# Feed-forward block products on Trainium2: one 512-column product for the high weights, and block products from an earlier pair

## The chip, the cores and the metric

The kernel runs on one core of one Trainium2 chip, in one launch. The metric is the device time of that launch in microseconds. Three runs of the kernel before took 1226.37, 1226.70 and 1227.45 us, median 1226.7. Shares, waits and durations come from one profiled execution of the same kernel. Engines are named as the profile has them: PE is TensorE (PEld its weight loads), DVE is VectorE, ACT is ScalarE, POOL is GpSimd, SP is SyncE, whose queue issues most of the DMAs.

## What is computed

Two layers of a decoder trunk on one sequence of 512 positions, 1024 wide, in float32. Layer 0 mixes tokens by a stick-breaking attention, layer 1 by a sparse attention that selects keys. Each layer ends in the gated feed-forward that the change is about:

```python
def conv_ffn(h, w_up, conv_w, conv_b, w_down):      # h (1, 512, 1024)
    S = h.shape[1]
    u = h @ w_up                                    # (1024, 2 * 2816)
    up = jnp.pad(u, ((0, 0), (CONV_W - 1, 0), (0, 0)))
    y = conv_b
    for j in range(CONV_W):
        y = y + up[:, j:j + S] * conv_w[j]
    gate, val = jnp.split(y, 2, axis=-1)
    return (jax.nn.silu(gate) * val) @ w_down       # (2816, 1024)
...
mod = cond @ ada_w[i] + ada_b[i]
sh1, sc1, g1, sh2, sc2, g2 = [m[:, None, :] for m in jnp.split(mod, 6, axis=-1)]
...
h = rms_norm(x, norm_ffn[i]) * (1.0 + sc2) + sh2
x = x + g2 * conv_ffn(h, ffn_w_up[i], ffn_conv_w[i], ffn_conv_b[i], ffn_w_down[i])
```

## The kernel before

**Numbers in two parts.** Every float32 operand of a large product is split into a high part (rounded to the matmul's type, `whi`, `hhi`, `thi`, `acthi`, `dnhi`) and the rest (`wlo`, `hlo`, ...). A product is three: high weight with high input, high weight with low input, low weight with high input. The high part of a weight is a ScalarE copy. The low part is either a VectorE subtraction, or a negated ScalarE copy onto which an accumulating DMA, issued by POOL, adds the float32 weight again (`neg_...`, `add_...`).

**Pairs.** Each feed-forward has 22 pairs j = 0 to 21: 128 columns of the gate half and 128 of the value half of `w_up`. A plain pair (`up_plain`, `plain_hi` and `plain_lo`, L1525 and L1529) makes two products of 512 positions: for each of the halves 8 row tiles of the weight times three, 48 matmuls of 512 columns.

**Seven products.** From pair `FIRST_7` on (12 in the first feed-forward, 7 in the second) a pair is made by seven block products in place of eight (`up_7`, `product`, L1549). The input is cut into four blocks, two halves of the 1024 features by two halves of 256 positions, the weight into four, two halves of the rows by gate and value. Sums of weight blocks (`sum13`, `sum24a`, `sum24b`) and of input blocks (the combinations T, `combos`, once per feed-forward) make seven products a1, a2, e, d1, d2, c1, c2. Each is 4 row tiles times three, 12 matmuls of 256 columns. They accumulate in three PSUM banks, and are read out between products: bank a takes a1, e, c1 and c2 on top of one another, and after a1 a ScalarE copy takes the gate's first half (`gate` 0), after e another copy (`x`), after c1 a VectorE addition (`val` 1), and after c2 a copy (`gate` 2). Bank b holds a2 (`gate` 1), bank d holds d1 and then d2 (`v`, and `val` 0). So a product that accumulates onto a bank has to wait until the one before has been read. The block's result then goes through scale, two convolution steps, silu and a multiplication into A[j].

**Down products.** `w_down` is multiplied in rounds over pairs 0-5, 6-11, 12-17 and 18-21. The first three rounds make 24 down products (`down`, L1624): six pairs of A times three, 18 matmuls of 512 columns, added to x by VectorE (L744). `DOWNS_7` says after which pair how many of them stand. In the seven-product pairs one stands between c1 and c2, so that TensorE has work while VectorE reads bank a, and the rest of them after c2.

**Dots.** The modulation vectors `mod` are computed on VectorE: 8 dots per vector (`dot`, L651) over loaded 512 KB chunks of `ada_w`, spread over the work as fillers. A bias (`bias_job`) takes one of the shift vectors out to DRAM, reads it back on all partitions (`shrow`), and makes two more dots with weight columns.

**What sets the order.** `ffn_plan` lists the jobs of a feed-forward with an estimated duration each, keeps TensorE's jobs in the order of the program, gives every other job a latest time by what waits for it, and runs a list schedule over the engines and the ring buffers. The result is the order in which instructions are issued. Each engine then works through its queue in that order and waits at semaphores. Tables steer the plan: `FIRST_7`, `DOWNS_7`, `ORDER_7` (the order of products in a pair), `PLAIN_DMA` and `DOWN_DMA` (which low parts come by accumulating DMA), `DOT_SPAN` and `LEADS`. Float32 weights are loaded into a ring of six `raw` buffers by SP.

Of the kernel before, what the change touches and what calls it, by code (L numbers as in the profile page):

```python
# [19 lines left out]
S = 512  # L20
P = 128
# [40 lines left out]
FIRST_7 = [12, 7]  # L62
DOWNS_7 = [[(6, 1), (7, 2), (8, 1), (9, 1), (10, 1), (11, 1), (12, 2), (13, 1), (14, 2), (15, 1), (16, 1), (17, 1), (18, 2),
            (19, 2), (20, 2), (21, 3)],
           [(6, 2), (7, 1), (8, 1), (9, 1), (10, 1), (11, 1), (12, 2), (13, 1), (14, 2), (15, 1), (16, 1), (17, 1), (18, 2),
            (19, 2), (20, 2), (21, 3)]]
ORDER_7 = ["a1", "d1", "a2", "e", "d2", "c1", "down", "c2", "rest"]
WEIGHT_7 = {"a1": 0, "d2": 0, "a2": 1, "d1": 13, "c1": 13, "e": 24, "c2": 24}
BANK_7 = {"a1": "a", "e": "a", "c1": "a", "c2": "a", "a2": "b", "d1": "d", "d2": "d"}
LATE_CHUNKS = [(2, 3), ()]  # L70
A_RING = 11
BIAS_AT = [16, 20, 26, 30]
LATE_DOTS = True
DOT_SPAN = [(0.0, 300.0), (5.0, 60.0)]
PLAIN_DMA = [(), [(j, i) for j in range(4, 7) for i in range(2)]]
DOWN_DMA = [(), ()]
LEADS = [dict(plain=14.0, r=20.0, sum=13.0, down=12.0, T=28.0, last=12.0, bias=2.0)] * 2
# [116 lines left out]
def ffn_dots(l):  # L194
    groups = [[(0, 5), (1, 0), (1, 3), (1, 1), (1, 2), (1, 4)] + ([] if LATE_DOTS else [(1, 5)]), [(1, 5)] if LATE_DOTS else []][l]
    jobs = [g + (f,) for g in groups for f in range(KT)]
    if l == 0:
        for n, at in zip((1, 1, 2, 2), BIAS_AT):
            jobs.insert(at, ("bias", n, "row" if ("bias", n, "col") in jobs else "col"))
    return jobs  # L200


def ffn_plan(l):
# [112 lines left out]
    def up_7(j, downs):  # L316
# [19 lines left out]
        done = {}  # L336
        for what in ORDER_7:
            if what in ("down", "rest"):
                for i in downs[:1] if what == "down" else downs:
                    down(i)  # L340
                downs = downs[1:]
                continue
            need = [done[n] for n in {"e": ["g0"], "d2": ["v"], "c1": ["x"], "c2": ["v1"]}.get(what, [])]
# [3 lines left out]
            m1 = p.add("PE", 8 * 0.12, "prod_hi", j, what, after=[hi] + need)  # L347
# [5 lines left out]
            if bank not in done:  # L353
                done[bank] = p.place("x" if what == "a2" else "mm", m1)

            def after(name, engine, us, fn, arg, *needs):
                if name not in done and all(n in done for n in needs):
                    done[name] = p.add(engine, us, fn, j, arg, after=[done[n] for n in needs])
                    return True

            if after("g0", "ACT", 0.38, "gate", 0, "a1"):
                gate = p.place("u", done["g0"])
            after("g1", "DVE", 0.42, "gate", 1, "g0", "a2")
            if after("v", "ACT", 0.38, "copy", "v", "d1"):
                small = p.place("sqt", done["v"])
            after("x", "ACT", 0.38, "copy", "x", "e", "v")
            if after("v1", "DVE", 0.42, "val", 1, "v", "c1"):
                val = p.place("u", done["v1"])
            after("v0", "DVE", 0.42, "val", 0, "x", "d2", "v1")
            after("g2", "ACT", 0.38, "gate", 2, "c2")  # L370
        small.users += [done["v1"], done["v0"]]
        done["bank a"].users.append(done["g2"])
        done["bank b"].users.append(done["g1"])
        done["bank d"].users.append(done["v0"])
        v = evacuate(j, 1, [done["v0"], done["v1"]])
        g = evacuate(j, 0, [done["g1"], done["g2"]])
        gate.users.append(g[0])
        val.users.append(v[0])
        mix(j, g, v)

    def down(i):
# [13 lines left out]
        bank = p.place("z" if m % 2 else "tr", m1)  # L395
        m2 = p.add("PE", 6 * 0.2266, "down", i, 1, after=[lo])
        w.users.append(m2)
        for j in ins:
            A[j][2].users.append(m2)
        bank.users.append(p.add("DVE", 0.75, "add", i, after=[m2] + gate_done))  # L400

    gate_done = []
# [3 lines left out]
    for d in jobs:  # L406
# [21 lines left out]
    assert n == 3 * KT  # L428
    for j in range(2, FT):
        if j == first:  # L430
            combos(p.t)
        if j >= first:
            up_7(j, downs.get(j, ()))
        else:
            up_plain(j)
            for i in downs.get(j, ()):
                down(i)
# [59 lines left out]
def kernel_body(ctx, tc, xT, wst, cst, smalls, crow, ccol, relb, outT):  # L497
# [126 lines left out]
    ada_cap = len(ada_jobs)  # L624
    tail = [(0, 5, f) for f in range(KT)] + [(1, g, f) for g in (1, 0, 3, 2, 4, 5) for f in range(KT)]
    for n, at in ((1, 29), (2, 42)):
        for d, what in ((0, "col"), (4, "row")):
            tail.insert(at + d, ("bias", n, what))
    ada_jobs += tail
    ada_state = {"i": 0, "cap": ada_cap}  # L630
# [130 lines left out]
    def boundary(n, last, O, l, gate, nxt, first, place, begin=None):  # L761

# [4 lines left out]
        norm_scale(nl, gcol, sc)  # L767
        fetch(pos["i"] + 1)
# [101 lines left out]
    def stick_layer(l):  # L870
        with ExitStack() as st:
# [497 lines left out]
            ada_finish()  # L1369
            ada_state["cap"] = len(ada_jobs)  # L1370
# [17 lines left out]
    def ffn_layer(l, first, man):  # L1388
        with ExitStack() as st:
# [45 lines left out]
            class do:  # L1435
# [66 lines left out]
                def combo_hi(k):  # L1502
                    T[k] = [fp.tile([P, 3 * H2], F32R, name=n, bufs=4) for n in ("thi", "tlo")]
# [69 lines left out]
                def val(j, i):  # L1573
                    if i == 1:
                        Y[j, "val"] = npool.tile([P, S], F32, name="val", tag="u", bufs=3)
                        dve.tensor_add(Y[j, "val"][:, H2:], half[j][:, :H2], pt[j, "a"])
# [800 lines left out]
```

## Time and profile before

| | us |
|---|---|
| median of three runs | 1226.7 |
| the profiled execution's own time | 1226.43 |
| its span, first to last instruction | 1224.6 |
| POOL busy | 171.2 |
| first feed-forward on TensorE | 280.3 to 588.1 |
| second feed-forward on TensorE | 894.9 to 1199.3 |

The page of the profile gives each engine's busy time, the chain of work that ended last, and the costliest groups of instructions. A row of a group names the line, the engine, the operation, output and input tiles with partitions x elements, and the count; behind the first bar the busy time in us and the mean ns of one, behind the second the idle time of the engine just before these instructions and what ended it. In rows in order of time the first number is the start, the second how long it took, both in us from the span's start, and a bracket gives the idle time ahead of it and what ended that. [...] Here are the totals that the prediction does not show again, of ScalarE's and VectorE's waits in the second feed-forward's seven-product part (957 to 1191 us):

```profile
ACT vx L1562 <- PE pt_a L1549: 26.1, 15, 2.5
...
DVE raw L1474 <- ACT whi L1442: 10.6, 10, 2.4
...
DVE x L744 <- PE pt_d L1624: 6.0, 12, 1.1
```

The three numbers are the total in us, how often, and the longest: both engines wait there for TensorE and for each other.

### The profile page before, as it was taken

The page shows a single profiled execution, that of the slowest core. Times are in us where ns is not written, and L with a number is a line of the kernel's source. Part 1 is how long each engine was busy: PE and PEld are TensorE (multiplying, and loading weights), DVE is VectorE, ACT ScalarE, POOL GpSimd, SP SyncE. Part 2 cuts the span into 40 slices and gives each one's busy share as a digit, 9 for nine tenths or more (in the row PEclk, how much of TensorE's full clock was granted, in tenths as well). Part 3 has the DMA queues.
Part 4 walks back from the last instruction along what each step waited for, and adds up shares of the span by engine and source line. Part 5 has one row for each costly group of instructions (what it writes and reads, how often), then busy time and mean ns, then how long its engine had stood idle before and what let it go on. Part 6 is the DMA issues. An engine that isn't in the chain of part 4 may idle for free.

```text
span 1224.6 us, 18659 instructions
## 1 busy us (share of the span) xinstructions
PE 1218.8 (100%) x6924; PEld 1036.2 (85%) x6924; DVE 1029.9 (84%) x1715; ACT 736.9 (60%) x1265; POOL 171.2 (14%) x187
## 2 busy tenths in 40 slices
PE   9999999999999999999999999999999999999998
PEld 6878787788888899999888778777888999999997
DVE  5899998899999999999888996666999988778763
ACT  5587667466434456755556457874686676656550
POOL 0000000000000001110001357774001011101000
PEclk9999999999999999999999999999999999999999
DMA  9665344524655778885522311142359677666621
GB/s 372 236 186 160 129 162 138 173 86 136 217 189 177 246 234 239 217 242 185 189 69 74 100 52 52 53 139 69 101 137 233 195 165 169 150 147 159 159 84 69
DMA packets 59020, 192.46 MB, mean 157 GB/s; under 512 B 6960, under 2 KB 7728, under 8 KB 58928
## 3 DMA queue, kind: packets, MB, share of 16 engines
q1 hardware_dynamic: 50400, 166.88, 41.4%
q0 software_dynamic: 8528, 24.39, 11.8%
q8 instruction: 54, 0.88, 0.3%
q14 instruction: 38, 0.31, 0.1%
HBM read 189.13 MB, written 2.11 MB: 156 GB/s over the span
## 4 chain that ended last, share of the span: by engine, by line
PE 93%; DVE 4%; DMA 1%; ACT 1%; issue 1%; SPq 0%; DVEq 0%; ACTq 0%
PE pt_d L1624 16%; PE pt_a L1549 12%; PE pt_u L1525 9%; PE pt_d L1549 6%; PE pt_u L1529 4%; PE pt_b L1549 3%; PE pt_q L617 2%; PE pt_q L619 2%; PE pt_q L618 2%; PE pt_qk L617 2%; PE pt_qk L618 2%; PE pt_qk L619 2%; PE pt_l L617 2%; PE pt_l L619 2%; PE pt_l L618 2%; PE av L2123 2%
## 5 line engine op out<-in xcount | busy, mean ns | idle before, releaser
L1624 PE MATMUL pt_d<-acthi,dnhi 128*128 128x512 f32 x288 | 112.5, 391 | 0.2 <-ACT dnhi L1605 0.2
L1624 PE MATMUL pt_d<-actlo,dnhi 128*128 128x512 f32 x288 | 112.6, 391 | 0.0
L1442 ACT ACTIVATE whi<-raw 128x1024 fp32r<-128x1024 f32 x72 | 75.8, 1056 | 57.1 <-PE pt_a L1549 30.2
L1454 POOL DMA_DIRECT2D wlo<-wst x31 | 26.8, 866 | 595.5 <-ACT wlo L1450 480.7
L1525 PE MATMUL pt_u<-hhi,whi 128*128 128x512 f32 x240 | 93.4, 389 | 0.0
L1525 PE MATMUL pt_u<-hlo,whi 128*128 128x512 f32 x240 | 93.4, 389 | 0.0
L567 ACT ACTIVATE whi<-raw 128x1024 fp32r<-128x1024 f32 x80 | 84.0, 1052 | 1.0 <-PE pt_o L619 0.8
L651 DVE SCALAR_TENSOR_TENSOR ada<-ada,cond 128x1024 f32<-128x1024 f32 x56 | 68.4, 1221 | 8.2 <-DMA ada<-wst 7.7
L1549 PE MATMUL pt_a<-hlo,whi 128*128 128x256 f32 x300 | 75.2, 283 | 0.0
L1549 PE MATMUL pt_a<-hhi,whi 128*128 128x256 f32 x300 | 74.9, 282 | 0.0
L576 DVE TENSOR_TENSOR wlo<-raw,whi 128x1024 fp32r<-128x1024 f32 x59 | 71.8, 1220 | 2.9 <-ACT whi L567 2.6
L1624 PE MATMUL pt_d<-acthi,dnlo 128*128 128x512 f32 x288 | 73.1, 389 | 0.0
L1624 PEld LDWEIGHTS pt_d<-acthi,dnlo 128*128 128x128 f32 x288 | 54.1, 188 | 11.2
L1624 PEld LDWEIGHTS pt_d<-acthi,dnhi 128*128 128x128 f32 x288 | 54.2, 188 | 10.5 <-ACT dnhi L1605 0.4
L1624 PEld LDWEIGHTS pt_d<-actlo,dnhi 128*128 128x128 f32 x288 | 54.2, 188 | 10.3
L1446 DVE TENSOR_TENSOR wlo<-raw,whi 128x1024 fp32r<-128x1024 f32 x41 | 50.1, 1223 | 13.6 <-ACT whi L1442 11.8
L1529 PE MATMUL pt_u<-hhi,wlo 128*128 128x512 f32 x240 | 59.3, 389 | 0.0
L1549 PEld LDWEIGHTS pt_a<-hlo,whi 128*128 128x128 f32 x300 | 57.4, 191 | 1.4
L1549 PEld LDWEIGHTS pt_a<-hhi,whi 128*128 128x128 f32 x300 | 57.3, 191 | 1.4
L1808 DVE CUSTOM_DVE_ANT_0 L<-z,L,cols 128x128 f32<-128x128 f32 (+3 forms) x60 | 32.5, 548 | 30.2 <-PE tr L2092 19.9
L576 POOL TENSOR_TENSOR wlo<-raw,whi 128x1024 fp32r<-128x1024 f32 x18 | 43.1, 2396 | 85.9 <-PE pt_q L618 46.1
L1264 DVE TENSOR_TENSOR_SCAN mz<-mz,diag 128x128 f32<-128x128 f32 (+1 forms) x64 | 52.4, 819 | 1.5 <-ACT mz L1259 1.4
(386 smaller groups left out, 3825.8 us busy)
## 6 DMA issues: line engine op xcount, KB each, us to landing
raw<-wst SPq DMA_DIRECT2D x200, 512.0 KB, 4.4
ada<-wst SPq DMA_DIRECT2D x60, 512.0 KB, 3.9
raw<-wst SPq DMA_DIRECT2D x48, 384.0 KB, 4.7
wlo<-wst POOLq DMA_DIRECT2D x34, 512.0 KB, 7.2
whi<-wst POOLq DMA_DIRECT2D x25, 256.0 KB, 4.9
th<-relb SPq DMA_DIRECT2D x16, 256.0 KB, 3.3
x<-xT SPq DMA_DIRECT2D x4, 512.0 KB, 5.1
shrow<-shd SPq DMA_DIRECT2D x3, 512.0 KB, 4.4
```

The lines of the kernel that those rows point to most:

```text
L567: act.activation(hi[:, :n], raw[:, :n], AF.Copy)
L576: engine.tensor_sub(lo[:, :w], raw[:, :w], hi[:, :w].bitcast(F32))
L617: pe.matmul(out, lhsT=whi, rhs=ahi, start=start, stop=False)
L618: pe.matmul(out, lhsT=wlo, rhs=ahi, start=False, stop=False)
L619: pe.matmul(out, lhsT=whi, rhs=alo, start=False, stop=stop)
L651: dve.scalar_tensor_tensor(raw, raw, 1.0, cond, op0=OP.mult, op1=OP.mult, accum_out=dst)
L1264: dve.tensor_tensor_scan(rev, rev, diag[:, S - ns:][:, ::-1], 0.0, OP.mult, OP.max)
L1442: act.activation(W[j, i][0], R[j, i], AF.Copy)
L1525: pe.matmul(pt[j, i], lhsT=W[j, i][0][:, k * P:(k + 1) * P], rhs=hs[k][n], start=k + n == 0, stop=False)
L1529: pe.matmul(pt[j, i], lhsT=W[j, i][1][:, k * P:(k + 1) * P], rhs=hs[k][0], start=False, stop=k == KT - 1)
L1549: pe.matmul(out, lhsT=w[:, c0 + k * P:c0 + (k + 1) * P], rhs=a[n], start=new and k + n == 0, stop=part == 1 and k == 3 and what in ("a2", ...
L1624: pe.matmul(pt["dn", i], lhsT=dn[i][part][:, k * P:(k + 1) * P], rhs=A[j0 + k][n], start=part + k + n == 0, stop=part == 1 and k == j1 - j ...
```

## The change

1. **Merged products.** High and low part of the input lie in one tile now (`hh`, `tt`), the low one behind the high one. For the pairs in `MERGED` (none in the first feed-forward; 7, 9, 10 and 12 to 21 in the second) the products of the high weight with both parts are one matmul of 512 columns: its input is 256 columns of the high part and 256 of the low part, its output the whole bank, whose second half (`side`) gathers the low input's share. Each time the bank's first half has been read, a VectorE addition (`side`) adds the second half too: six a pair.
2. **Seven products from pair 8** in the first feed-forward in place of 12.
3. **Order.** A down product is now two jobs, its high part (12 matmuls) and its low part (6). In the second feed-forward the high part stands ahead of c1 and the low part between c1 and c2; in the first the two still stand together ahead of c2. Down products use the two banks "z" alone, and bank d moves to "tr".
4. **Low parts by DMA.** 12 down weights in the first feed-forward and 14 in the second get their low part by accumulating DMA (none before); of the plain pairs' weights five in the first (none before) and five in the second (six before).
5. **Dots.** The last three dots of layer 1's scale vector and the second feed-forward's bias move from the first feed-forward into the end of the sparse attention (`late_dots`, and `after_scale` in `boundary`). Spans, leads and counts of down products are other numbers.

```diff
-FIRST_7 = [12, 7]
+FIRST_7 = [8, 7]
-ORDER_7 = ["a1", "d1", "a2", "e", "d2", "c1", "down", "c2", "rest"]
+ORDER_7 = [['a1', 'd1', 'a2', 'e', 'd2', 'c1', 'down', 'low', 'c2', 'rest'],
+           ['a1', 'd1', 'a2', 'e', 'd2', 'down', 'c1', 'low', 'c2', 'rest']]
-PLAIN_DMA = [(), [(j, i) for j in range(4, 7) for i in range(2)]]
-DOWN_DMA = [(), ()]
+PLAIN_DMA = [[(4, 0), (4, 1), (6, 1), (7, 0), (7, 1)], [(4, 0), (4, 1), (5, 0), (5, 1), (6, 0)]]
+DOWN_DMA = [[1, 3, 4, 5, 6, 7, 9, 12, 13, 16, 19, 21], [0, 1, 3, 4, 7, 9, 10, 11, 12, 14, 15, 16, 19, 23]]
+LATE_DOTS = [(1, 4, 5), (1, 4, 6), (1, 4, 7)]
+MERGED = [[], [7, 9, 10, 12, 13, 14, 15, 16, 17, 18, 19, 20, 21]]
...
     def new_h():
-        hcur["h"] = [(hpool.tile([P, S], F32R, name="hhi"), hpool.tile([P, S], F32R, name="hlo"))
-                     for _ in range(KT)]
+        both = [hpool.tile([P, 2 * S], F32R, name="hh") for _ in range(KT)]
+        hcur["h"] = [(t[:, :S], t[:, S:]) for t in both]
+        hcur["both"] = [t.rearrange("p (n c) -> p n c", n=2) for t in both]
...
                     for k in range(4):
                         a = do.operand(what, k)
+                        if part == 0 and j in MERGED[l]:
+                            pe.matmul(pt[j, bank, "both"], lhsT=w[:, c0 + k * P:c0 + (k + 1) * P], rhs=a[2], start=new and k == 0,
+                                      stop=False, skip_group_check=True)
+                            continue
                         for n in range(2 - part):
...
+                def side(j, what, bank):
+                    t, c = {"g": (Y.get((j, "gate")), slice(0, H2)), "h": (Y.get((j, "gate")), slice(H2, S)),
+                            "v": (half.get(j), slice(0, H2)), "x": (half.get(j), slice(H2, S)),
+                            "v0": (Y.get((j, "val")), slice(0, H2)), "v1": (Y.get((j, "val")), slice(H2, S))}[what]
+                    dve.tensor_add(t[:, c], t[:, c], pt[j, bank, "side"])
...
+                    if h == HEADS - 2:
+                        late_dots(2)
+                    if not more:
+                        late_dots(1)
...
+                    if h == HEADS - 4:
+                        load_dots(3)
+                        bias_job(2, "col")
...
+                                 after_scale=lambda: bias_job(2, "row"))
```

What this moves, first on TensorE, in the second feed-forward, between c1 and c2 of one of the last pairs. Before, the end of the down product that stands there, and c2 (`pt_a`):

```order
L1624 MATMUL pt_d<-acthi,dnlo 128x512 x6
L1549 MATMUL pt_a<-hhi,whi 128x256
L1549 MATMUL pt_a<-hlo,whi 128x256
L1549 MATMUL pt_a<-hhi,whi 128x256
L1549 MATMUL pt_a<-hlo,whi 128x256
L1549 MATMUL pt_a<-hhi,whi 128x256
L1549 MATMUL pt_a<-hlo,whi 128x256
L1549 MATMUL pt_a<-hhi,whi 128x256
L1549 MATMUL pt_a<-hlo,whi 128x256
L1549 MATMUL pt_a<-hhi,wlo 128x256 x4
```

And now, from c1 over the down product's low part and c2 to the next pair's a1:

```order
L1583 MATMUL pt_a<-hh,whi 128x512 x4
L1587 MATMUL pt_a<-hh,wlo 128x256 x4
L1669 MATMUL pt_d<-acthi,dnlo 128x512 x6
L1583 MATMUL pt_a<-hh,whi 128x512 x4
L1587 MATMUL pt_a<-hh,wlo 128x256 x4
```

Eight matmuls of 256 columns have become four of 512, and of the down product's 18 only the last six are left between c1 and c2.

Second, on VectorE at the same place, a pair's read-outs around `val` of bank a. Before (`raw` and `s` are the next pair's weight sums, `wlo` a low part, `y` the convolution):

```order
L1569 TENSOR_TENSOR gate<-gate,pt_b 128x256 [waits PE_49]
L1474 TENSOR_TENSOR raw<-s_11777,raw 128x512 [waits Activation_49]
L1477 TENSOR_TENSOR raw<-raw 128x512 [waits DVE_49]
L1576 TENSOR_TENSOR val<-vx,pt_a 128x256 [waits PE_49]
L1578 TENSOR_TENSOR val<-vx,pt_d 128x256
L1446 TENSOR_TENSOR wlo<-s_11777,whi 128x1024 [waits DMASW0_49,Activation_49]
```

And now, in pair 14 (L1615 is `val` of bank a, L1617 of bank d, L1607 `gate` of bank b, L1623 a `side`, L1504 and L1507 the sums, L1476 a low part):

```order
L1617 TENSOR_TENSOR val<-vx,pt_d 128x256 [waits DVE_49,PE_49]
L1623 TENSOR_TENSOR val<-val,pt_d 128x256
L1504 TENSOR_TENSOR raw<-s_10849,raw 128x512 [waits Activation_49]
L1607 TENSOR_TENSOR gate<-gate,pt_b 128x256
L1507 TENSOR_TENSOR raw<-raw 128x512 [waits DVE_49]
L1435 SCALAR_TENSOR_TENSOR y_10895<-val,sm,y_10895 128x511 [waits Activation_49]
L1623 TENSOR_TENSOR gate<-gate,pt_b 128x256 [waits DVE_49]
L1615 TENSOR_TENSOR val<-vx,pt_a 128x256 [waits PE_49]
L1623 TENSOR_TENSOR val<-val,pt_a 128x256 [waits DVE_49]
L1476 TENSOR_TENSOR wlo<-s_10849,whi 128x1024 [waits DMASW1_49,Activation_49]
L1435 SCALAR_TENSOR_TENSOR y_10895<-val,sm,y_10895 128x510
L774 SCALAR_TENSOR_TENSOR x_89<-pt_d,mod_88,x_89 128x512 [waits PE_49]
```

Each read-out is followed by a `side`, bank d is read ahead of bank a, and c2 has the `side` behind L1615 to wait for where it had `val` itself.

Third, on VectorE near the end of the sparse attention: two of the late dots (L680) between an addition to x and the softmax row L1850 of the last heads.

```order
L774 SCALAR_TENSOR_TENSOR x_91<-pt_o,mod_88,x_91 128x512
L680 SCALAR_TENSOR_TENSOR raw,mod_88<-raw,cond 128x1024 [waits DMAHW7_49,DMAHW1_49]
L680 SCALAR_TENSOR_TENSOR raw,mod_88<-raw,cond 128x1024 [waits DMAHW6_49,DMAHW2_49,DMAHW0_49]
L1850 ISA L_8633,nm<-z,L_8633,cols 128x384 [waits PE_49,Pool_49]
L1850 ISA nm 128x1
```

Before, L1850's row followed the addition to x directly; now two loads from DRAM have to have landed first.

More of the change, by code (lines that the diff above doesn't have):

```diff
@@ L314, in combos, with up_7 @@
         p.add("DVE", 0.1, "negate", due=t - 2)
-    def up_7(j, downs):
+    def up_7(j, downs, before):
         t = p.t
@@ L335, in up_7, with then, product @@
         downs = list(downs)
[L336 to L343, printed above, removed]
+        done, place = {}, {}
+        merged = j in MERGED[l]
+        s_ = "s" if merged else ""
+        def then(name, engine, us, fn, arg, needs, ring=None, side=None):
+            if name in done or not all(n in done for n in needs):
+                return
+            done[name] = p.add(engine, us, fn, j, arg, after=[done[n] for n in needs])
+            if ring and ring[0] not in place:
+                place[ring[0]] = p.place(ring[1], done[name])
+            if merged:
+                done[name + "s"] = p.add("DVE", 0.42, "side", j, *side, after=[done[name]])
+        def product(what):
+            need = [done[n + s_] for n in {"e": ["g0"], "d2": ["v"], "c1": ["x"], "c2": ["v1"]}.get(what, [])]
             if what in ("d1", "d2", "e", "c1"):
@@ L352, in up_7 @@
             bank = "bank " + BANK_7[what]
[L353 to L379, printed above, removed]
+            if bank not in place:
+                place[bank] = p.place(TAG_7[bank[5:]], m1)
+            then("g0", "ACT", 0.38, "gate", 0, ["a1"], ("gate", "u"), ("g", "a"))
@@ new lines, in product @@
+            then("g1", "DVE", 0.42, "gate", 1, ["g0" + s_, "a2"], None, ("g", "b"))
+            then("v", "ACT", 0.38, "copy", "v", ["d1"], ("small", "sqt"), ("v", "d"))
+            then("x", "ACT", 0.38, "copy", "x", ["e", "v"], None, ("x", "a"))
+            then("v0", "DVE", 0.42, "val", 0, ["x" + s_, "d2"], ("val", "u"), ("v0", "d"))
+            then("v1", "DVE", 0.42, "val", 1, ["v" + s_, "c1", "v0"], None, ("v1", "a"))
+            then("g2", "ACT", 0.38, "gate", 2, ["c2"], None, ("h", "a"))
@@ new lines, in up_7 @@
+        for what in ORDER_7[l]:
+            if what == "before":
+                if before:
+                    before()
+            elif what == "down":
+                low.extend(down(i) for i in downs[:1])
+                downs = downs[1:]
+            elif what == "low":
+                if low:
+                    low.pop()()
+            elif what == "rest":
+                for i in downs:
+                    down(i)()
+                downs = []
+            elif what == "c2":
+                finish()
+            else:
+                product(what)
@@ L394, in down, with low @@
         m1 = p.add("PE", 12 * 0.2266, "down", i, 0, after=[hi] + [x for j in ins for x in A[j][:2]])
[L395 to L402, printed above, removed]
+        bank = p.place("z", m1)
+        def low():
+            m2 = p.add("PE", 6 * 0.2266, "down", i, 1, after=[lo])
+            w.users.append(m2)
+            for j in ins:
+                A[j][2].users.append(m2)
+            bank.users.append(p.add("DVE", 0.75, "add", i, after=[m2] + gate_done))
+        return low
+    gate_done, low = [], []
     jobs = ffn_dots(l)
@@ L436, in ffn_plan @@
             for i in downs.get(j, ()):
-                down(i)
+                down(i)()
+    if "before" in ORDER_7[l]:
+        left()
+    for f in low:
+        f()
     for m in range(4):
@@ L623, in kernel_body @@
         ada_jobs.insert(at, ("bias", 0, what))
[L624 to L630, printed above, removed]
+    ada_state = {"i": 0, "cap": len(ada_jobs)}
     shifts = {}
@@ L1541, in product @@
                     if new:
-                        pt[j, bank] = ptile([P, S], "pt_" + bank, "x" if what == "a2" else "mm")[:, :H2]
+                        t = ptile([P, S], "pt_" + bank, TAG_7[bank])
+                        pt[j, bank], pt[j, bank, "side"] = t[:, :H2], t[:, H2:]
+                        pt[j, bank, "both"] = t.rearrange("p (n c) -> p n c", n=2)
                     out = pt[j, bank]
@@ L2049, in follow, with load_dots, late_dots @@
                         events.pop(0)
+                raw_dots = []
+                def load_dots(n):
+                    raw_dots.extend((d, chunk_raw(("ada",) + d)) for d in LATE_DOTS[len(raw_dots):][:n])
+                def late_dots(n):
+                    for _ in range(n):
+                        (_, g, f), raw = raw_dots.pop(0)
+                        ada_dot(mod[l][:, g * KT + f:g * KT + f + 1], raw)
+                        if f == KT - 1:
+                            ada_sum(l, g)
                 def masked_bias(h, j):
```

79 lines of the change are left out of this document (48 added, 31 removed).

## Prediction

> **What bounds the kernel now.** I read the page first, for the engines' shares and the chain that ended last, and then the list of what TensorE waited for.
>
> ```profile
> span 1224.6 us, 18659 instructions
> PE 1218.8 (100%) x6924; PEld 1036.2 (85%) x6924; DVE 1029.9 (84%) x1715; ACT 736.9 (60%) x1265; POOL 171.2 (14%) x187
> PE 93%; DVE 4%; DMA 1%; ACT 1%; issue 1%; SPq 0%; DVEq 0%; ACTq 0%
> ...
> PE pt_idle L902 <- DVE ecols L523: 1.0, 1, 1.0
> ...
> PE pt_d L1624 <- ACT dnhi L1605: 0.2, 1, 0.2
> ```
>
> TensorE is busy all the time, and the second wait quoted is the only one it has in either feed-forward. But a matmul's row lasts longer than its share of the stream, since the next one starts under it, so "busy" alone could hide a slow stream. The chain in order of time gives the pace: each piece ends where the next begins.
>
> ```profile
> 280.27 3.63 PE pt_u L1525 x16
> 283.90 1.81 PE pt_u L1529 x8
> ...
> 498.17 1.44 PE pt_d L1549 x12
> ...
> 579.93 8.19 PE pt_d L1624 x36
> ...
> 894.86 3.63 PE pt_u L1525 x16
> ...
> 1191.10 8.19 PE pt_d L1624 x36
> ```
>
> A 512-column matmul takes 3.63/16 = 0.2267 us, a 256-column one 1.44/12 = 0.120. So a plain pair (48 of 512 columns) takes 10.88 us, a pair of seven products (84 of 256) 10.08, a down product (18 of 512) 4.08. The first feed-forward should take 10 x 10.88 + 10 x 10.08 + 24 x 4.08 = 307.5 us, and takes 280.27 to 588.12, 307.85. The second, 5 x 10.88 + 15 x 10.08 + 24 x 4.08 = 303.5, takes 894.86 to 1199.29, 304.4. Both run at the pace of the matmuls to within 1 us: **time goes where TensorE's stream goes**, as long as VectorE, ScalarE and the DMAs keep ahead of it. How far ahead they are shows in the busy times by stage:
>
> ```profile
> core 0: us, PE busy (x) PEld busy (x) DVE busy (x) ACT busy (x) POOL busy (x), PEclk, DMA share, GB/s
> ...
> 280.00:334.00 54.00, 54.00 (x240) 44.74 (x239) 50.16 (x70) 32.58 (x43) 0.00 (x0) 1.00 0.58 186
> 334.00:417.00 83.00, 83.00 (x367) 68.74 (x367) 76.49 (x120) 35.50 (x47) 1.72 (x2) 1.00 0.60 188
> 417.00:588.00 171.00, 171.00 (x1150) 158.60 (x1149) 157.42 (x236) 100.95 (x153) 15.54 (x18) 1.00 0.80 236
> ...
> 950.00:1191.00 241.00, 240.78 (x1654) 224.83 (x1653) 192.58 (x267) 153.31 (x235) 24.18 (x28) 1.00 0.64 155
> ```
>
> VectorE is 92% busy over the first feed-forward's 308 us, and 80% in the second's seven-product part. TensorE's clock is granted in full.
>
> **The change, part by part.** *First feed-forward, pairs 8 to 11.* Four pairs go from 10.88 to 10.08: 4 x 0.80 = **-3.2 us** of stream.
>
> *Second, merged products.* In 13 of the 15 pairs each of the 7 x 4 pairs of 256-column matmuls (high weight with high, then with low input) becomes one of 512: 2 x 0.120 - 0.2267 = 0.0133 us each, 13 x 28 = 364 of them, **-4.85 us**. The 512-column operand is now two pieces of 256 lying apart; no row shows such a one. Bounds: nothing gained (it costs two of 256), or the 0.2267 of every contiguous 512-column row. I take the latter, the nearest row, whose width and output bank are the same.
>
> [...]
>
> *VectorE.* Six additions of the low-input half per merged pair, 78 in all, each like "val" here:
>
> ```profile
> L651 DVE SCALAR_TENSOR_TENSOR ada<-ada,cond 128x1024 f32<-128x1024 f32 x26 | 31.7, 1220 | 1.3 <-DMA ada<-wst 1.2
> L1608 DVE TENSOR_TENSOR dnlo<-raw,dnhi 128x768 fp32r<-128x768 f32 x17 | 16.2, 955 | 2.7 <-ACT dnhi L1605 2.5 <-issue 0.3
> ...
> L1446 DVE TENSOR_TENSOR wlo<-raw,whi 128x1024 fp32r<-128x1024 f32 x9 | 11.0, 1224 | 3.5 <-ACT whi L1442 3.4
> ...
> L1576 DVE TENSOR_TENSOR val<-vx,pt_a 128x256 f32<-128x256 f32 x10 | 4.2, 420 | 4.3 <-PE pt_a L1549 4.1
> ...
> L1605 ACT ACTIVATE dnhi<-raw 128x768 fp32r<-128x768 f32 x16 | 13.4, 838 | 8.5 <-PE pt_d L1624 6.5 <-DMA raw<-wst 1.4 <-PE pt_a L1549 0.7
> ```
>
> Second: 78 x 0.42 = +32.8, less 14 down splits (14 x 0.955 = 13.4) that go to ScalarE and an accumulating DMA, plus one plain split 1.2: +20.6. 192.6 + 20.6 = 213 of 236 us, **90%, as the first has now** with TensorE never waiting for VectorE. First: a seven-product pair has 3.9 us more on VectorE than a plain one (a sum of 1.2 like wlo's, two of 0.69 as in the rows at 1007.60 and 1008.32 below, three of 0.42), x4 = +15.4; off go 12 down splits 11.5, 5 plain splits 6.1, 3 dots 3.9 and two bias dots 2.6: -8.7. ScalarE gains 14 x 0.84 in the second, some 35 in the first, and stays at 70% or below. All of it lies beside the stream. Uncovered, the 20.6 alone would turn the result.
>
> *The tightest cover.* A merged pair's last product (c2) overwrites the bank that VectorE has to read twice first (val, then the low half). Between c1 and c2 stood a whole down product, 4.08 us; now only its low part, 6 x 0.2267 = 1.36. What the handover takes:
>
> ```profile
> 1022.62 0.64 PE L1549 MATMUL pt_a<-hhi,wlo 128*128 128x256 f32 x4
> 1023.10 0.40 PE L1624 MATMUL pt_d<-acthi,dnhi 128*128 128x512 f32 x1
> ...
> 1007.60 0.69 DVE L1474 TENSOR_TENSOR raw<-s,raw 128x512 f32<-128x512 f32 x1 [1.25 <-ACT whi L1442]
> 1008.32 0.69 DVE L1477 TENSOR_TENSOR raw<-raw 128x512 f32<-128x512 f32 x1
> ...
> 1023.30 0.42 DVE L1576 TENSOR_TENSOR val<-vx,pt_a 128x256 f32<-128x256 f32 x1 [0.30 <-PE pt_a L1549]
> 1023.64 0.69 DVE L1477 TENSOR_TENSOR raw<-raw 128x512 f32<-128x512 f32 x1
> ```
>
> The down product starts at 1023.10, where c1's stream ends, and val at 1023.30: 0.20. A dependent instruction follows 0.03 after the end (1007.60 + 0.69 to 1008.32), an independent one starts 0.08 before it (1023.64). So val and side end at 0.20 + 0.42 + 0.03 + 0.42 = 1.07. The way back to TensorE is in no row; between 0 and the 0.20 of the way there it leaves 0.1 to 0.3 of the 1.36. Queued behind val are its side, a weight split and an addition to x, which have until the next pair. What stands ahead decides: one split still running (1.2) makes c2 about 1 us late. Over 13 pairs: 0 to 13 us. VectorE's overlapping starts give it some 0.08 us per row, over 1 us a pair, that its busy share does not show as free; so I take the near end, **+0.8 us**, four waits like the 0.2 above.
>
> *Moved to the sparse attention.* Three dots and the second bias. At the 1.22 of L651, two dots before the wait at 837.06, one (with the 8-column sum behind it) before 843.96, two bias dots before 855.37:
>
> ```profile
> 832.66 0.75 DVE L744 SCALAR_TENSOR_TENSOR x<-pt_o,mod,x 128x512 f32<-128x512 f32 x1
> 837.06 0.62 DVE L1808 CUSTOM_DVE_ANT_0 L<-z,L,cols 128x384 f32<-128x384 f32 x1 [3.65 <-PE z L1798]
> ...
> 843.96 1.02 DVE L2099 COPY pT<-tr 128x512 f32<-128x512 f32 x2 [2.10 <-PE tr L2092]
> ...
> 855.37 1.43 DVE L744 SCALAR_TENSOR_TENSOR x<-pt_l,mod,x 128x512 f32<-128x512 f32 x2 [2.63 <-PE pt_l L619]
> ```
>
> 2 x 1.3 = 2.6 in 3.65, 1.5 in 2.10, 2.6 in 2.63: nothing, or up to 6.7 if their loads are late, since they stand in VectorE's queue ahead of the softmax rows and of x. On SP's queue the six extra loads go ahead of the next projections' weights. I take 0.
>
> *DMA.* Accumulating transfers are dear:
>
> ```profile
> q1 hardware_dynamic: 9782, 33.00, 55.3%
> q0 software_dynamic: 2592, 7.08, 24.3%
> ...
> wlo<-wst POOLq DMA_DIRECT2D x9, 512.0 KB, 7.0
> ```
>
> Of these 171 us a loaded MB takes 0.553 x 171/33.0 = 2.87 us of all 16 engines, an accumulated one 5.87. A pair of 8 to 11 in the first feed-forward, with its down product and two dots, loads 2.50 MB (7.2 us) and accumulates 1.18 (6.9): **14.1 of its 14.16 us**, where the plain stage had a share of 0.60. Over the whole first feed-forward 10.5 MB more accumulated and 3.1 less loaded make 218 us of share into 271 of 305. That is full for four pairs, with room behind. Taken at 0, since loads run ahead into six buffers; bounds 0 and the price below.
>
> [...]
>
> **Sum.** The profiled execution took 1226.4 us (span 1224.6 and 1.8 around it; the median of the runs is 1226.7): 1226.4 - 3.2 - 4.85 + 0.8 = **1219.2**.
>
> **Rivals.** *A, the forecast*, TensorE-bound, 1217.6 to 1221.
>
> *B, VectorE late for c2.* It arrives half a split late in most of the 13 pairs: about 0.45 x 13 = 5.9 more, 1225. For: 0.1 to 0.3 of margin, 90% load, an in-order queue. Against: the val quoted starts 0.20 after c1, on time, and the first feed-forward ran at 92% without a wait.
>
> *D, the change does not do what it says:* two pieces cost two matmuls, or what is fixed in a matmul is hardly there to be saved. Then little but the four pairs gains: 1226.4 - 3.2 + 0.8 = 1224.0, or somewhat less. For: no row of such an operand. Against: the rows of 256 and of 512 both take their columns and 13 ns. [...]
>
> *C, DMA-bound in pairs 8 to 11, the slower side.* If transfers under this load take a quarter longer, a pair needs 17.6 instead of 14.16: 4 x 3.5 = 14, giving 1226.4 - 8.05 + 14 = 1232. They cost the gain from 8.05/(4 x 14.1), some 14%, on. For: the full share. Against: the stage with a share of 0.80 has no wait of TensorE for a split.
>
> **How the numbers follow.** A 0.66, B 0.17, D 0.06, C 0.11 (a third of it mild, a stall of 2 to 6 us). The likeliest gives 1219.2. The range runs from 1217.6 (no stall, and the 0.9 us lost now gone too) to 1224.5, which takes in D and half of B, and leaves out the rest of B and most of C. A measurement here tells about 0.2%, 2.45 us, from no change. Faster: A, D and over half of B, 0.82; same 0.09; slower 0.09, C's heavy part and B's worst.
>
> **What would show it.** Merged products 0.2267 us apart (D: 0.24); the second feed-forward near 299.5 us, the first near 304.5; TensorE's list of waits without the side additions (B: 0.3 us or more at c2, 13 times) and without low weight parts in 330 to 420 us (C); nothing new at 830 to 890. I am wrong if c2 waits for VectorE in most pairs, or if the DMA share stands at 1.0 from pair 8 on with waits for wlo.

## Result: slower by 0.6%, a gain in one feed-forward and a larger loss in the other

| | before | after |
|---|---|---|
| median, us | 1226.6 | 1235.0 |
| lowest to highest, us (4 runs each) | 1226.4 to 1227.5 | 1232.0 to 1236.3 |
| profiled execution's own time | 1226.4 | 1234.6 |
| first feed-forward on TensorE | 307.85 | 320.0 |
| second feed-forward on TensorE | 304.4 | 300.5 |

The ratio is 1.0064, 95% interval 1.0044 to 1.0083. The forecast was 1219.2.

From the page of the profile after, the engines' busy times, and the chain that ended last by engine and by line:

```profile
PE 1217.6 (99%) x6704; PEld 1024.9 (83%) x6704; DVE 1048.4 (85%) x1800; ACT 772.5 (63%) x1327; POOL 205.2 (17%) x225
PE 78%; DMA 10%; DVE 8%; issue 2%; ACT 1%; SPq 0%; DVEq 0%; ACTq 0%
PE pt_d L1669 11%; PE pt_a L1587 6%; DMA ada<-wst 5%; PE pt_u L1556 5%; DMA raw<-wst 4%; PE pt_a L1583 4%; PE pt_d L1587 3%; PE pt_q L652 2%; PE pt_q L654 2%; PE pt_q L653 2%; PE pt_u L1560 2%; PE pt_qk L652 2%; PE pt_qk L653 2%; PE pt_qk L654 2%; PE pt_d L1583 2%
```

The busy share of TensorE has hardly moved. The chain has: 93% of it was TensorE, now 78%, and 10% are loads, nearly all of two kinds, the dots' (`ada`) and the weights' (`raw`). Where it happened shows in the chain in order of time: the last down products of the first feed-forward, the start of the second, and its end.

```profile
592.12 8.19 PE pt_d L1669 x36
...
907.03 3.63 PE pt_u L1556 x16
...
1199.33 8.19 PE pt_d L1669 x36
```

The first feed-forward starts at 280.3 as before and ends at 592.12 + 8.19 = 600.31: 12.2 us more, where 3.2 less was forecast, so 15.4 us are lost in it. From there to the second it is 306.72 us, against 306.74 before. The second takes 1207.52 - 907.03 = 300.49, 3.94 less than before.

TensorE's waits in the first feed-forward, with those of ScalarE and VectorE for loads (total us, times, longest):

```profile
DVE ada L680 <- DMA ada<-wst: 25.0, 20, 5.4
...
ACT dnhi L1650 <- DMA raw<-wst: 19.2, 10, 5.1
...
PE pt_a L1587 <- ACT vx L1600: 6.8, 4, 4.2
...
PE pt_a L1587 <- ACT gate L1609: 1.7, 1, 1.7
...
PE pt_d L1587 <- ACT vx L1600: 0.8, 1, 0.8
```

TensorE waits 9.3 us, always for a small ScalarE copy of a bank. ScalarE in turn waited 19.2 us for down weights, and VectorE 25.0 us for the dots' chunks. The longest of these waits, read engine by engine. First SP's queue (start, length of the piece with its waits inside, what it issued), then VectorE:

```profile
484.12 10.18 SPq L1689 DMA_DIRECT2D ada<-wst  x2
494.39 1.49 SPq L571 DMA_DIRECT2D raw<-wst  x3
```

```profile
492.72 1.22 DVE L680 SCALAR_TENSOR_TENSOR ada<-ada,cond 128x1024 f32<-128x1024 f32 x1
```

Then ScalarE and TensorE:

```profile
500.30 0.84 ACT L1650 ACTIVATE dnhi<-raw 128x768 fp32r<-128x768 f32 x1 [1.73 <-DMA raw<-wst]
501.04 0.37 ACT L1600 ACTIVATE vx<-pt_a 128x256 f32<-128x256 f32 x1
```

```profile
501.46 2.08 PE L1587 MATMUL pt_a<-hh,whi 128*128 128x256 f32 x8 [4.16 <-ACT vx L1600]
...
504.19 0.63 PE L1669 MATMUL pt_d<-acthi,dnhi 128*128 128x512 f32 x1
504.62 0.63 PE L1669 MATMUL pt_d<-actlo,dnhi 128*128 128x512 f32 x1
...
508.04 0.39 PE L1669 MATMUL pt_d<-acthi,dnhi 128*128 128x512 f32 x1
508.27 0.39 PE L1669 MATMUL pt_d<-actlo,dnhi 128*128 128x512 f32 x1
```

Read backwards: TensorE stands until 501.46 for the copy `vx`, whose input it had finished some 4 us earlier. The copy stands behind the split of a down weight, `dnhi`, that begins at 500.30 when its load has landed. That load was issued from 494.39 on. Ahead of it on SP's queue stood the load of the next dot's chunk, and that one waited until the dot before had left the one buffer, at 493.9. This dot did not wait for its own load, which had landed: VectorE goes to it at 492.72 without idle time, but late. After the wait TensorE steps at 0.43 us a matmul of 512 columns (504.19 to 504.62) until about 507.6, then at 0.23 again. So the wait costs 4.16 us and about 3 more behind it. The granted clock by stage (same columns as in the prediction) shows it too, and the two engines' load:

```profile
440.00:480.00 40.00, 38.33 (x242) 35.46 (x243) 35.23 (x54) 23.89 (x37) 6.95 (x8) 0.96 0.91 254
480.00:520.00 40.00, 35.84 (x241) 33.55 (x240) 31.60 (x48) 22.80 (x36) 4.32 (x5) 0.91 0.80 228
...
280.00:600.00 320.00, 310.74 (x1898) 280.38 (x1897) 275.66 (x419) 196.57 (x292) 38.87 (x45) 0.98 0.82 226
...
957.00:1199.00 242.00, 242.00 (x1311) 209.43 (x1310) 215.03 (x351) 160.75 (x248) 33.73 (x39) 1.00 0.73 175
```

40 x 0.04 + 40 x 0.09 = 5.2 us of clock. Some 0.4 of it lie inside the wait that ends at 501.46, since the clock stands at 0.86 from 500 to 501 us and at 0.50 from there on. So the 9.3 us of waits and the clock together make 14.1 of the 15.4; the other 1.3 are not traced.

### The profile page after: what moved, and what is told of

It reads as the page before. It is cut to its first block, busy times and chain, and to the rows that moved or that the text cites. A ratio compares the mean times of both kernels' runs of the same rounds, so it can differ in the third digit from the quotient of the medians.

```text
span 1232.9 us, 18478 instructions
## 1 busy us (share of the span) xinstructions
PE 1217.6 (99%) x6704; PEld 1024.9 (83%) x6704; DVE 1048.4 (85%) x1800; ACT 772.5 (63%) x1327; POOL 205.2 (17%) x225
## 4 chain that ended last, share of the span: by engine, by line
PE 78%; DMA 10%; DVE 8%; issue 2%; ACT 1%; SPq 0%; DVEq 0%; ACTq 0%
PE pt_d L1669 11%; PE pt_a L1587 6%; DMA ada<-wst 5%; PE pt_u L1556 5%; DMA raw<-wst 4%; PE pt_a L1583 4%; PE pt_d L1587 3%; PE pt_q L652 2%; PE pt_q L654 2%; PE pt_q L653 2%; PE pt_u L1560 2%; PE pt_qk L652 2%; PE pt_qk L653 2%; PE pt_qk L654 2%; PE pt_d L1583 2%
## 5 line engine op out<-in xcount | busy, mean ns | idle before, releaser
L1484 POOL DMA_DIRECT2D wlo<-wst x39 | 33.8, 865 | 465.9 <-DVE ada L680 267.5
L680 DVE SCALAR_TENSOR_TENSOR ada<-ada,cond 128x1024 f32<-128x1024 f32 x53 | 64.7, 1221 | 26.9 <-DMA ada<-wst 26.7
L1556 PE MATMUL pt_u<-hh,whi 128*128 128x512 f32 x352 | 83.4, 389 | 0.0
L1556 PEld LDWEIGHTS pt_u<-hh,whi 128*128 128x128 f32 x352 | 66.1, 188 | 13.7
L611 DVE TENSOR_TENSOR wlo<-raw,whi 128x1024 fp32r<-128x1024 f32 x59 | 71.8, 1219 | 3.0 <-ACT whi L602 2.6
L1587 PE MATMUL pt_a<-hh,whi 128*128 128x256 f32 x384 | 55.0, 287 | 6.8 <-ACT vx L1600 6.8
L1587 PEld LDWEIGHTS pt_a<-hh,whi 128*128 128x128 f32 x384 | 51.7, 194 | 9.4 <-ACT vx L1600 7.6
L1587 PE MATMUL pt_a<-hh,wlo 128*128 128x256 f32 x348 | 56.0, 284 | 0.0
L1850 DVE CUSTOM_DVE_ANT_0 L<-z,L,cols 128x128 f32<-128x128 f32 (+3 forms) x60 | 32.5, 547 | 26.2 <-PE tr L2146 19.9
L1650 ACT ACTIVATE dnhi<-raw 128x768 fp32r<-128x768 f32 x48 | 40.2, 836 | 21.4 <-DMA raw<-wst 19.2
L1587 PEld LDWEIGHTS pt_a<-hh,wlo 128*128 128x128 f32 x348 | 50.8, 192 | 3.1
L652 PE MATMUL pt_q<-hh,whi 128*128 128x512 f32 x128 | 52.0, 406 | 0.0
```

Of the source, the lines that this page charges most:

```text
L611: engine.tensor_sub(lo[:, :w], raw[:, :w], hi[:, :w].bitcast(F32))
L652: pe.matmul(out, lhsT=whi, rhs=ahi, start=start, stop=False)
L680: dve.scalar_tensor_tensor(raw, raw, 1.0, cond, op0=OP.mult, op1=OP.mult, accum_out=dst)
L1556: pe.matmul(pt[j, i], lhsT=W[j, i][0][:, k * P:(k + 1) * P], rhs=hs[k][n], start=k + n == 0, stop=False)
L1587: pe.matmul(out, lhsT=w[:, c0 + k * P:c0 + (k + 1) * P], rhs=a[n], start=new and k + n == 0, stop=part == 1 and k == 3 and what in ("a2", ...
```

## Experiments

Three theories on the 15.4 us were set against each other. **T1**: the accumulating transfers fill the DMA engines, as rival C had it. **T2**: the order of SP's queue. A dot's load has one buffer and waits for the dot before it, and the weights behind it on the queue come late; its two halves are the weights held up on SP (T2a), and VectorE standing at a dot whose load is late (T2b). **T3**: the four more pairs of seven products load VectorE and ScalarE too much. A time marked "single run" is that of one run; run to run the changed kernel scatters by over 4 us, so such differences carry weight from about 5 us on or together with their traces. Each kernel is the changed one with the lines shown.

**1. The second feed-forward's change alone.**

```diff
+FIRST_7[0] = 12
+DOT_SPAN[0] = (0.0, 300.0)
+PLAIN_DMA[0] = []
+DOWN_DMA[0] = []
+LEADS[0] = dict(plain=14.0, r=20.0, sum=13.0, down=12.0, T=28.0, last=12.0, bias=2.0)
+DOWNS_7[0] = [(6, 1), (7, 2), (8, 1), (9, 1), (10, 1), (11, 1), (12, 2), (13, 1), ...
```

> The second feed-forward as changed (merged products), the first with the tables of before (seven products from pair 12, no accumulated low parts but for the sums). All three theories on the first feed-forward say the same here: its stalls go, it takes 307.9 us again, the second keeps its 300.5, total 1222 to 1223. If the total stays near 1235, the loss is not in the first feed-forward's tables.

Measured: 1222.2 (7 runs), ratio to before 0.9968 (0.9956 to 0.9979). As expected: the loss is all in the first feed-forward's tables, and the rest of the change is worth 4 us.

**2. No accumulated low parts of plain and down weights in the first feed-forward.**

```diff
+PLAIN_DMA[0] = []
+DOWN_DMA[0] = []
```

> The changed kernel, but no low part by accumulating DMA for plain and down weights in the first feed-forward (VectorE subtracts them again, 17.6 us more for it). T1, the transfers fill the DMA engines: the stalls go, first feed-forward 304.5 to 306, total 1219 to 1221. T2, SP's queue stands behind loads that wait for dots, and ScalarE and VectorE stand in order behind weights that come late: landings are shorter, but the queue is as it was, about half of the 15 us stays, total 1225 to 1230. T3, the seven-product pairs load VectorE and ScalarE too much: VectorE has more to do, total 1235 or over.

Measured: 1226.4 (single run), some 8 us back, 7 above the forecast. That is in T2's range and in neither of the others', but VectorE has more to do as well: it is 294 of 320 us busy. The dots' loads land in 3.7 us again, yet TensorE still waits 3.8 us. This run alone tells nothing apart; runs 8 and 9 add to it.

**3. Seven products from pair 12, the accumulated low parts kept.**

```diff
+FIRST_7[0] = 12
+DOWNS_7[0] = [(6, 1), (7, 2), (8, 1), (9, 1), (10, 1), (11, 1), (12, 2), (13, 1), ...
```

> The changed kernel, but with seven products from pair 12 in the first feed-forward, as before; its 17 accumulated low parts, leads and dot span stay. T1: four pairs' accumulated halves (1.5 MB a pair more for sums) are gone, transfers fit, 308 to 311 us for the first feed-forward, total 1223 to 1226. T2: the queue is as it was, stalls of 5 to 15 us, total 1227 to 1237. T3: no stall, 307.9, total 1222.5.

Measured: 1227.0 (single run), 4.8 above run 1, at the edge of T1's and T2's ranges. Against T3 alone: TensorE waits 2.3 us without the four pairs. The leads and the span of the dots are the changed ones here; no run changes them alone.

**4. The first feed-forward's dots read no chunk, their loads are still made.** The kernel leaves out what these dots compute.

```diff
-                    ada_dot(mod[n][:, g * KT + f:g * KT + f + 1], R[n, g, f])
+                    if l == 0:
+                        dve.scalar_tensor_tensor(cond, cond, 1.0, cond, op0=OP.mult, op1=OP.max, accum_out=mod[n][:, g * KT + f:g * KT + f + 1])
+                    else:
+                        ada_dot(mod[n][:, g * KT + f:g * KT + f + 1], R[n, g, f])
```

> The changed kernel, but the first feed-forward's dots no longer read the loaded chunk: every load of ada_w is still made, and VectorE does a pass of the same size over cond (the modulation vectors computed there are not the reference's). T1: as many bytes move, the stalls stay, total 1232 to 1236. T2: SP no longer waits for a dot ahead of a load and VectorE no longer for a load ahead of a dot, 10 to 15 us come back, total 1219 to 1225. T3: nothing changes, 1235.

Measured: 1221.3 (single run), 13.7 below the changed kernel's median. From its trace, the end of the first feed-forward, and the stage 440 to 480 us by engine:

```profile
578.90 8.19 PE pt_d L1669 x36
```

```profile
440.00:480.00 40.00, 38.05 (x252) 34.81 (x252) 33.97 (x51) 24.98 (x38) 6.09 (x7) 1.00 0.96 270
```

The first feed-forward starts at 280.14 here and takes 587.09 - 280.14 = 306.95 us. The same bytes moved, with the DMA engines at 0.96 in this stage, more than in the changed kernel: T1 falls as the main cause. But the run takes away both halves of T2 at once.

**5. The same, but SP waits for the dots again**, by a store of 128 x 4 bytes of each dot's result ahead of the next load. **6. The control**, the same stores of a tile that is always ready. The store in run 5, and in run 6:

```diff
+nc.sync.dma_start(junk["t"][:, junk["n"]:junk["n"] + 1], mod[n0][:, c:c + 1])
+nc.sync.dma_start(junk["t"][:, junk["n"]:junk["n"] + 1], sm[:, c:c + 1])
```

> As in the run where the dots don't read the loaded chunk (VectorE never waits for a load of ada_w; 1221.3), but SP waits for every dot again: ahead of each load it stores that dot's result (128 x 4 bytes) to DRAM. T2a, SP's queue held up behind dots makes the weights late: the stalls come back, 1229 to 1236. T2b, VectorE standing in order at dots whose load is late is what costs: 1220 to 1224.

> The control for the run in which SP waits for the dots (1231.0): the same dots that read no chunk, the same 44 small stores on SP's queue ahead of the loads, but of a tile that is always ready, so SP waits for no dot. T2a, the wait for the dot is what costs: 1220 to 1223.5. If the small stores themselves cost, 1228 or over.

Measured: 1231.0 with the wait, 1221.0 without (single runs): SP's wait for the dots alone brings back 10 of the 13.7 us. By the traces the first feed-forward takes 315.5 and 306.4 us. In run 5's trace, SP's wait for the dots and TensorE's longest wait, of the same kind and at nearly the same time as the changed kernel's (there 4.16 us at 501):

```profile
SPq L1692 <- DVE cond L1700: 159.9, 36, 10.2
```

```profile
498.84 2.08 PE L1588 MATMUL pt_a<-hh,whi 128*128 128x256 f32 x8 [5.15 <-ACT vx L1601]
```

In run 6 SP stands too, but for the load before to land in the one buffer:

```profile
SPq L1696 <- DMA ada<-wst: 130.7, 31, 8.3
```

So what costs here is not that SP stands behind one buffer, but that it stands behind VectorE's work. T2a holds in this form. T2b is left with the 4 us to the changed kernel's median at most, which is within the scatter of single runs.

**7. The dots' buffer joins the weights' six in a ring of seven.** The memory is the same; a dot's load may go 8 us of the plan earlier, so the order of issue moves too.

```diff
+ADA_LEAD = 8.0
-    for name, places in (("raw", 6), ("whi", 4), ("wlo", 4), ("dn", 2), ("y0", 2), ("y1", 2), ("u", 3), ("sqt", 2),
+    for name, places in (("raw", 7), ("whi", 4), ("wlo", 4), ("dn", 2), ("y0", 2), ("y1", 2), ("u", 3), ("sqt", 2),
-            got, raw = load("load_ada", *d, ring="ada", key=due)
+            got, raw = load("load_ada", *d, key=due - ADA_LEAD)
-    raws = ctx.enter_context(tc.tile_pool(name="raws", bufs=6))
+    raws = ctx.enter_context(tc.tile_pool(name="raws", bufs=7))
-                    R[d] = fp.tile([P, D], F32, name="ada", bufs=1)
+                    R[d] = raws.tile([P, D], F32, name="ada", tag="raw")
```

> The changed kernel, but the one buffer of the dots' loads joins the six weight buffers to a ring of seven, so a dot's load can be issued up to 8 us of the plan ahead, with no wait for the dot before it. T1 (bytes): stalls stay, 1230 to 1236. T2 (one buffer: load, dot, load in a loop): most of the stalls go, 1219 to 1224.

Measured: 1220.8 (4 runs), ratio to before 0.9953 (0.9938 to 0.9968). This is the change with its loss mended, and the fastest kernel here that leaves nothing out; its interval overlaps that of run 1. The end of its first feed-forward, the stage 440 to 480 us, and the dots on VectorE:

```profile
577.78 8.19 PE pt_d L1670 x36
```

```profile
440.00:480.00 40.00, 39.26 (x258) 35.80 (x257) 34.98 (x53) 25.72 (x39) 6.78 (x8) 1.00 1.00 295
```

```profile
L681 DVE SCALAR_TENSOR_TENSOR ada<-ada,cond 128x1024 f32<-128x1024 f32 x53 | 64.5, 1218 | 0.4 <-DMA ada<-wst 0.3
```

The first feed-forward goes from 280.19 to 585.97, 305.8 us, 1.1 over the 304.65 of the forecast's steps. The DMA engines stand at 1.00 for 40 us, and TensorE waits 0.74 us. The dots' idle time of 26.9 us on VectorE is down to 0.4.

**8. Seven products from pair 8 with low parts made by VectorE and the leads and span of before. 9. Run 7 with these.**

```diff
+DOT_SPAN[0] = (0.0, 300.0)
+PLAIN_DMA[0] = []
+DOWN_DMA[0] = []
+LEADS[0] = dict(plain=14.0, r=20.0, sum=13.0, down=12.0, T=28.0, last=12.0, bias=2.0)
```

> The changed kernel with seven products from pair 8 in the first feed-forward, but with the leads, the dot span and the VectorE-made low parts of before there. T1: no accumulated low parts but the sums' halves, transfers fit, 1219 to 1221. T2: landings are short as before, the loop keeps up, 1219 to 1223. T3: VectorE has 15 us more in the first feed-forward than before, at 96% of it, and is late for bank a: 1226 or over.

> Seven products from pair 8 with the VectorE-made low parts, leads and dot span of before in the first feed-forward (1229.3 with one buffer for the dots), now with the ring of seven. T2: the stalls go, 1219 to 1222. T3, VectorE at some 96% is late for bank a: 1225 or over.

Measured: 1229.3 (single run) and 1232.6 (4 runs), the latter's ratio to before 1.0044 (1.0029 to 1.0059). Here T2 fails and T3 holds: the ring of seven helps nothing. From run 9, the stage 400 to 440 us, one of TensorE's waits, and VectorE ahead of what it waits for:

```profile
400.00:440.00 40.00, 34.18 (x225) 31.04 (x224) 38.44 (x59) 25.72 (x39) 3.46 (x4) 0.96 0.82 247
```

```profile
431.65 1.21 PE L1592 MATMUL pt_a<-hh,whi 128*128 128x256 f32 x8 [3.08 <-DVE val L1620]
```

```profile
427.65 1.22 DVE L1714 SCALAR_TENSOR_TENSOR raw<-raw,shrow 128x1024 f32<-128x1024 f32 x1
...
428.80 1.53 DVE L1440 SCALAR_TENSOR_TENSOR y<-val,sm,y 128x511 f32<-128x511 f32 x2
...
430.58 0.68 DVE L1640 TENSOR_TENSOR y<-y,y 128x512 f32<-128x512 f32 x1
431.18 0.41 DVE L1620 TENSOR_TENSOR val<-vx,pt_a 128x256 f32<-128x256 f32 x1
```

VectorE is busy 38.4 of 40 us and goes from row to row without a gap; the `val` that TensorE waits for stands behind a bias dot, two convolution steps and the product of the halves. So with the leads and the span of before the four pairs lose by VectorE when its low parts are not accumulated. Run 2, without accumulated parts but with the changed leads, was 3 us faster than run 8, and run 2 with the ring of seven was not made: whether the accumulated low parts are needed stays open.

**10. Longer landings in the plan.**

```diff
-return p.add("DMA", us, None, after=[s], lag=2.0), p.place(ring, s, key)
+return p.add("DMA", us, None, after=[s], lag=4.0), p.place(ring, s, key)
-after=[p.add("POOL", 0.87, fn, *args, after=after)], lag=3.0)
+after=[p.add("POOL", 0.87, fn, *args, after=after)], lag=5.0)
```

> The changed kernel with one thing else in the plan: a load is taken to land 4 us after its transfer time in place of 2, an accumulated one 5 in place of 3 (5.5 and 8 us for 512 KB, as the trace shows). Only the order of instructions moves. T1: no gain, 1231 to 1236. T2: loads are issued earlier and dots stand later in VectorE's queue, half or more of the stalls go, 1221 to 1228; but the dots' loop itself, one buffer, is no faster.

Measured: 1283.9 (4 runs), ratio 1.0467 (1.0449 to 1.0484). A miss for both theories: the plan, told the landing times that the trace shows, made a far worse order, with single waits of TensorE of 14.2 us for a `dnhi` and 16.7 us for a `whi` behind the feed-forward's end. Why is not settled; it says nothing on T1 or T2.

**11. Run 7 without merged products.**

```diff
+MERGED[1] = []
```

> The ring of seven (1220.8), without the merged products: every pair of the second feed-forward makes high and low input products of 256 columns apart, with no side additions. By the forecast (13 ns saved in each of 364 matmuls, less 0.8 of waits) it is 4.0 us slower, 1224.4 to 1225.7. [...]

Measured: 1224.9 (10 runs), ratio to before 0.9986 (0.9976 to 0.9995): 4.04 above run 7. The last down products of both feed-forwards, of this run and of run 7:

```profile
577.96 8.19 PE pt_d L1671 x36
...
1189.30 8.19 PE pt_d L1671 x36
```

```profile
1185.28 8.19 PE pt_d L1670 x36
```

611.34 us from end to end, against 1185.28 - 577.78 = 607.50: 3.84 of the 4.04 lie behind the first feed-forward's end.

**12. As run 4, without the loads.**

```diff
                 def load_ada(*d):
+                    if l == 0:
+                        return
```

> The changed kernel, first feed-forward's dots with neither load nor chunk: a VectorE pass of the same size over cond, and 22 MB less to load. Against the run that makes the loads without waiting for them (1221.3), the difference is what the bytes alone cost: by T1 the rest of the forecast is there, 1218 to 1219.5; if bytes cost nothing, 1221 again.

Measured: 1219.6 (single run). The end of its first feed-forward:

```profile
576.74 8.19 PE pt_d L1669 x36
```

From 280.23 that makes 304.70 us, against the forecast's 304.65. Against run 4 the dots' loads cost 2.25 us by the traces: no more than that is their share of T1.

## Why the prediction was wrong, step by step

**The stream's price, right.** Four pairs at -0.80 us each make 304.65 us; run 12 has 304.70.

**Merged products, right in sum.** -4.85 and +0.8 make -4.05; the second feed-forward took 3.94 less, and run 11 gives 4.04. Both terms were a little large, and that they cancel is luck: a merge saved some 11 ns (4.04 us over 364), not 13.3 (2 x 0.120 - 0.2267, from two rows), and the waits took nothing. TensorE's starts at two products of a merged pair (the first row lasts 1.07 us and the next starts 0.91 after it, so the pace is read from starts):

```profile
1103.45 1.07 PE L1583 MATMUL pt_a<-hh,whi 128*128 128x512 f32 x4
1104.36 0.64 PE L1587 MATMUL pt_a<-hh,wlo 128*128 128x256 f32 x4
1104.83 1.09 PE L1583 MATMUL pt_d<-tt,whi 128*128 128x512 f32 x4
1105.76 0.63 PE L1587 MATMUL pt_d<-tt,wlo 128*128 128x256 f32 x4
```

0.91/4 = 0.2275 and 0.93/4 = 0.2325, not 0.2267; and TensorE has no wait for a bank in the second feed-forward, so the four waits of 0.2 did not come. Rivals B and D fall. The cover of c2 by the rows of TensorE and VectorE there:

```profile
1114.57 1.55 PE L1669 MATMUL pt_d<-acthi,dnlo 128*128 128x512 f32 x6
1115.96 1.07 PE L1583 MATMUL pt_a<-hh,whi 128*128 128x512 f32 x4
```

```profile
1114.77 0.42 DVE L1615 TENSOR_TENSOR val<-vx,pt_a 128x256 f32<-128x256 f32 x1 [0.84 <-PE pt_a L1587]
1115.22 0.42 DVE L1623 TENSOR_TENSOR val<-val,pt_a 128x256 f32<-128x256 f32 x1
```

The `side` ends 1115.64 - 1114.57 = 1.07 after c1, as worked out, and c2 follows at 1.39 without waiting.

**VectorE, right.** 215.0 us in the second feed-forward's seven-product part, 213 forecast; 275.7 in the first, 8.4 less than the 284.1 before, 8.7 forecast. **Sparse attention, right:** the 0 held, 306.72 against 306.74 us.

**The step that failed: DMA, "Taken at 0, since loads run ahead into six buffers".** The step weighed bytes against the engines' time, and that part was about right: in pairs 8 to 11 (358 to 414 us) the DMA engines stand at 0.96, and TensorE waits 1.3 us. But the loads could not run ahead: on SP's queue they stand behind the dots' loads, and each of those waits for VectorE to finish the dot before. SP's waits for the dots (total us, times, longest) in the first feed-forward, before and after:

```profile
SPq L1644 <- DVE ada L651: 176.0, 41, 8.1
```

```profile
SPq L1689 <- DVE ada L680: 186.0, 35, 9.6
```

So SP stood there before as well, without a wait of TensorE. What is new is that the work behind it has no time to spare. The landing rows of the first feed-forward of both kernels (times issued, KB each, median us), before and after, show what moved:

```profile
ada<-wst SPq DMA_DIRECT2D x47, 512.0 KB, 3.8
```

```profile
ada<-wst SPq DMA_DIRECT2D x43, 512.0 KB, 5.3
raw<-wst SPq DMA_DIRECT2D x38, 512.0 KB, 6.7
wlo<-wst POOLq DMA_DIRECT2D x19, 512.0 KB, 8.1
```

With one buffer a dot takes its load and its own 1.22 us: before, 47 x (3.8 + 1.22) = 236 of 308 us; now, with the 45 dots that VectorE makes there, 45 x (5.3 + 1.22) = 293 of the forecast's 305, which leaves some 0.3 us a dot for VectorE to reach it. When this slack is used up, the weights behind it, ScalarE's splits of them, and the copies behind the splits are late in turn. The 293 are an estimate from medians, and they are not the whole cause: 20 of the 45 dots waited for their loads, but the dot behind the longest wait did not, and in run 5, where no dot waits for a load, SP's wait costs 9 us all the same. Shown by runs 5 to 7 is that SP's wait for VectorE's dots makes the loss. How it divides between longer landings and VectorE coming late for other reasons stays open.

**Rival C had the time by luck, not the mechanism.** Its 1232 came from 3.5 us in each of the pairs 8 to 11 for want of bandwidth. Runs 4 and 7 move the same bytes and lose 2.3 and 1.1 us; the largest waits, 1.73 and 4.16 us at 442 and 501 us, lie behind these pairs; and pairs 8 to 11 themselves (some 358 to 414 us) have two waits, 0.8 and 0.5 us. A rival on SP's queue was missing, though the order of that queue and the dots' single buffer could be read before the run.

**VectorE as the bound**, rival B's kind, exists, but in the first feed-forward, and, of the runs here, most plainly where its low parts are not accumulated (run 9). The changed tables buy VectorE's time with DMA time, and lose it on SP's queue.

## What to carry to other kernels

When transfers get longer, don't only add up their bytes: go along the queue that issues them, and for each load that waits for a buffer work out how often landing plus use fits into the stage, and how late the engine that has to free the buffer may come; whatever stands behind that load waits with it. A filler with a single buffer at the head of an in-order queue held up work here that has nothing to do with it (1231.0 us in run 5, 1221.0 in run 6), and one ring shared with the main loads mended it at no cost in memory (1220.8 in run 7). And a short wait of TensorE cost more than its length here: one of 4.16 us cost about 7, with a granted clock of 0.50 for some 6 us behind it.

## What was unexpected in the hardware

After the wait of 4.16 us TensorE ran at 0.43 us per 512-column matmul for some 6 us, and after one of 1.73 us the granted clock stood at 0.50 from 443 to 446 us, so that the 40 us stage around it had 0.96; the waits of 0.5 to 1.3 us left it at 1.00 in theirs. The 0.43 go with a granted clock of 0.50 (501 to 507 us), the forecast's 0.2267 with one of 1.00. The length of the wait does not decide alone: in run 4 one of 1.95 us left the clock at 1.00 in the same stage. What else decides is not shown.

Accumulated transfers of 512 KB landed in 8.1 us in the median (6.8 before, when there were 10 in place of 19). The dots' plain loads beside them landed in 5.3, against 3.8 before and 3.7 in run 2, which has no accumulated plain and down parts. The weights' loads went from 5.4 to 6.7, but took 6.6 in run 2 too, so that rise is not shown to come from the accumulated transfers.
